# Two column blocks of a down projection as one unit of seven block products: a float32 decoder block on one core

## The chip, the cores and the metric

The kernel runs on one core of one Trainium2 chip. The metric is the device time of one execution in microseconds (us). The kernel before was run three times: 2167.27 us median, 2163.76 to 2168.08. A core has TensorE (PE, matrix products), VectorE (DVE, element by element), ScalarE (ACT, functions and copies with a scale), GpSimd (POOL) and SyncE (SP, here the queue that issues nearly all DMAs).

## The reference, cut to what matters

One decoder layer over 256 tokens of width 2048, in float32: a half-step FFN, a mixer (retention and sliding-window attention side by side), cross-attention into 256 memory tokens, a second half-step FFN, a final norm.

```
def swiglu(x, w_gate, w_up, w_down):
    return (jax.nn.silu(x @ w_gate) * (x @ w_up)) @ w_down
...
h = h + 0.5 * swiglu(rms_norm(h, ffn1_norm[l]), ffn1_w_gate[l], ffn1_w_up[l], ffn1_w_down[l])
n = rms_norm(h, mix_norm[l])
rq, rk, rv, rg, sq, sk, sv = jnp.split(n @ w_in[l], IN_SPLITS, axis=-1)
...
h = h + jnp.concatenate([ret, swa.astype(h.dtype)], axis=-1) @ w_out[l]
h = h + memory_cross_attention(rms_norm(h, xa_norm[l]), rms_norm(mem, mem_norm[l]), xa_wq[l], xa_wkv[l], xa_wo[l])
h = h + 0.5 * swiglu(rms_norm(h, ffn2_norm[l]), ffn2_w_gate[l], ffn2_w_up[l], ffn2_w_down[l])
return rms_norm(h, final_norm)
```

The inner width of an FFN is 5632, that is 11 blocks of 512; the model width is 4 blocks of 512.

## The kernel before, in words

**A product.** Each float32 operand is split into a high part (a rounded copy, made by ScalarE) and a low part (the rest, a subtraction on VectorE): `halves`, lines 74 to 77. `three` (lines 583 to 587) adds high x high, high x low and low x high into PSUM. The stationary operand is a 128x128 piece of the activations, the moving one a 128x512 piece of weights. The page's lines L585, L586 and L587 are these three matmuls, L72 the high part and L77 the low part of anything.

**Units and steps.** A `Unit` (lines 155 to 174) makes one block of 512 output columns for all 256 tokens. It goes over blocks of 512 of the inner dimension, two steps to a block; a step has two pieces of 128 rows, two halves of the tokens and three matmuls: 12 matmuls of 512 columns. All units stand in one list (`units`), and `run_stream` (lines 341 to 457) turns that list into one list of steps and runs it in order. `together` (lines 286 to 302) lets two neighbours run joined: both without their last block, then both last blocks. Ahead of each step the weights of the step three further on are split (`LOOKAHEAD`), and loads are issued up to four steps beyond that (`AHEAD`). Loads come by SP's queue, in the order of the program, into tiles `wf` (three buffers, each two steps); the splits lie in `wh` and `wl` (four buffers each).

**Twins and the seven products.** A `Twin` (lines 176 to 259) makes two blocks of columns, here gate and up of one FFN block, over the same activations. Three of the four inner blocks go by plain steps: 3 x 2 x 2 = 12. The fourth, number `SEVEN` = 3, is taken as 2x2 blocks (token half by rows) times 2x2 (rows by gate and up), which needs eight products by the rule and seven by a scheme of sums and differences: `prepare` (line 207) makes the differences of weights (L212) and their split, `multiply` (line 217) runs one of seven products of 6 matmuls; four of them use sums of activations (`sums_of`, lines 261 to 284; L277), and the results are put together by additions on VectorE (L238). The seven are put between the plain steps, from the third to the ninth. The two weight tiles of the fourth block ("wide") are `blk` tiles, 13 of which are shared by nearly everything else.

**The turn.** What a unit gives has tokens on partitions; the next product needs them on the free axis. `cross` (lines 556 to 575): VectorE transposes 32x32 pieces (L563) into a tile `t4k` (two buffers), one step later SP writes it to DRAM (`box`), two steps later GpSimd issues four reads back (L572), and `TURN` = 6 steps later a function receives the block: it makes halves of it, or adds it to the residual `hT` (L596). These delays count steps (`clock`; a product of the seven counts half): `later` puts a task in a list, and `run_due` runs it when its step comes. `run_until` runs tasks before their time when a step needs what they make.

**The FFN.** `ffn` (lines 612 to 663) goes over groups of blocks: all gate and up products of a group, then `down` for the group, which adds into the residual. The first block of an FFN (b = 0) is two units, the others are Twins. FFN1 has two groups, of 6 and 5 blocks; FFN2 has three, of 4, 4 and 3. `down` is four units, one for each block of columns, over the blocks of the group. FFN1's (`to_h`, lines 590 to 610) are scaled by 0.5 on ScalarE and crossed; FFN2's (lines 1105 to 1117) need no turn, since by then the residual has been turned back into two `blk` tiles (`turn_h`, line 1092), and they are added there by VectorE (L1116). A group's last block is due in the first down unit.

**Start.** PE runs a few products with the identity (L94, `WARM`) while the first loads are under way. The first 16 steps take a gate step and an up step in turn; the first weights come in pieces of 256 or 512 columns (lines 346 to 357).

## Time and profile before

| | |
|---|---|
| median of 3 runs | 2167.27 us (2163.76 to 2168.08) |
| the profiled execution | 2163.22 us |
| its span, first to last instruction | 2161.2 us |
| mean granted TensorE clock | 0.997 |
| busy share PE / DVE / ACT / POOL | 99% / 72% / 51% / 7% |
| matmuls | 9652 |
| read from HBM | 443.08 MB |

The profile shows one execution. Busy time of PE comes from modelled ends of pipelined matmuls, so a PE that is busy 99% needn't be at its best rate: the count of matmuls in a stretch says more. A line in the views is a line of the kernel; since helpers record most instructions, L72 and L77 stand for copies and splits of many tiles, and the tile's name (out<-in) tells which. The chain of waits gives start, length and who, each piece released by the one before it.

### The profile page before, as it was taken

Reading aid. Unit: us, or ns where it says so; the run is one execution under the profiler, and the core shown is the slowest. Engines: PE = TensorE matmul, PEld = TensorE weight load, DVE = VectorE, ACT = ScalarE, POOL = GpSimd, SP = SyncE. Lnnn points to the kernel's source line nnn. Section 1 sums busy time; section 2 is a strip of 40 time slices with the busy share of each in tenths; the row PEclk is TensorE's granted clock in tenths of the full one; section 3 lists DMA queues with packets and bytes.
Section 4 is the critical chain, followed back from the end, with each engine's and each line's share of the span. In section 5 each row is a group of like instructions: output and inputs, shape, how many; then the busy total and the mean of one; then the engine's idle time right before and its main releaser. Section 6 shows DMA issues by size and latency. Waiting matters only on the chain.

```text
span 2161.2 us, 25375 instructions
## 1 busy us (share of the span) xinstructions
PE 2142.7 (99%) x9652; PEld 1773.1 (82%) x9652; DVE 1548.7 (72%) x1827; ACT 1106.0 (51%) x1350; POOL 149.1 (7%) x257
## 2 busy tenths in 40 slices
PE   9999999999999999999999999999999999999998
PEld 7788888888888888888888888888888888888876
DVE  6888855688866678787675565567885688757865
ACT  6555544455545555646454544455554455535544
POOL 0000000000000010101111100010110000000000
PEclk9999999999999999999999999999999999999999
DMA  8666677666667566656867764585866566665663
GB/s 293 209 229 216 212 234 228 230 224 234 214 226 252 205 212 217 196 193 238 263 231 243 227 217 170 203 252 213 276 224 223 213 235 215 211 211 201 227 197 141
DMA packets 137531, 478.29 MB, mean 221 GB/s; under 512 B 11713, under 2 KB 12481, under 8 KB 137281
## 3 DMA queue, kind: packets, MB, share of 16 engines
q1 hardware_dynamic: 125600, 445.03, 58.9%
q0 software_dynamic: 11520, 31.47, 6.5%
q8 instruction: 75, 1.23, 0.2%
q14 instruction: 48, 0.39, 0.1%
q10 hardware_dynamic: 288, 0.18, 0.0%
HBM read 443.08 MB, written 33.55 MB: 221 GB/s over the span
## 4 chain that ended last, share of the span: by engine, by line
PE 92%; DMA 3%; DVE 2%; issue 1%; ACT 1%; POOL 0%; SPq 0%; ACTq 0%; POOLq 0%; DVEq 0%
PE acc L585 28%; PE acc L586 28%; PE acc L587 28%; DMA t4k<-box 2%; PE tmp L585 2%; PE tmp L586 2%; PE tmp L587 2%; DVE wl L77 1%; DMA wf<-in_w_in_rqk 0%; DMA box<-t4k 0%; POOL t4k L572 0%; DMA wf<-in_ffn_w_up 0%; PE tmp L810 0%; ACT blk L72 0%; PE tmp L791 0%
## 5 line engine op out<-in xcount | busy, mean ns | idle before, releaser
L77 DVE TENSOR_TENSOR wl<-wf,wh 128x1024 fp32r<-128x1024 f32 (+1 forms) x696 | 844.5, 1217 | 484.8 <-ACT wh L72 479.4
L72 ACT ACTIVATE wh<-wf 128x1024 fp32r<-128x1024 f32 (+1 forms) x696 | 732.0, 1055 | 809.7 <-PE acc L587 761.5
L585 PE MATMUL acc<-wh,blk 128*128 128x512 f32 (+1 forms) x2904 | 1131.3, 390 | 5.4 <-ACT blk L72 4.0
L586 PE MATMUL acc<-wl,blk 128*128 128x512 f32 (+1 forms) x2904 | 1128.8, 389 | 2.5 <-DVE wl L77 2.5
L587 PE MATMUL acc<-wh,blk 128*128 128x512 f32 (+1 forms) x2904 | 1128.2, 389 | 0.0
L585 PEld LDWEIGHTS acc<-wh,blk 128*128 128x128 f32 x2904 | 546.2, 188 | 121.8 <-ACT blk L72 5.4
L586 PEld LDWEIGHTS acc<-wl,blk 128*128 128x128 f32 x2904 | 546.3, 188 | 114.4 <-DVE wl L77 3.8
L587 PEld LDWEIGHTS acc<-wh,blk 128*128 128x128 f32 x2904 | 546.1, 188 | 112.7 <-DVE blk L77 0.6
L572 POOL DMA_DIRECT2D t4k<-box x240 | 138.6, 584 | 1790.6 <-DMA box<-t4k 549.7
L72 ACT ACTIVATE wh<-blk 128x1024 fp32r<-128x1024 f32 x140 | 148.3, 1060 | 78.4 <-PE acc L587 60.6
L77 DVE TENSOR_TENSOR wl<-blk,wh 128x1024 fp32r<-128x1024 f32 x140 | 170.6, 1218 | 8.7 <-ACT wh L72 3.2
L72 ACT ACTIVATE blk<-t4k 128x512 fp32r<-128x512 f32 (+3 forms) x84 | 46.6, 602 | 64.0 <-DMA t4k<-box 63.8
L212 DVE TENSOR_TENSOR blk<-blk,blk 128x1024 f32<-128x1024 f32 x60 | 73.4, 1224 | 1.4
L563 DVE STREAM_TRANSPOSE t4k<-t2k 128x512 f32<-128x512 f32 x88 | 57.7, 691 | 13.9 <-ACT t2k L72 13.8
L77 DVE TENSOR_TENSOR blk<-t4k,blk 128x512 fp32r<-128x512 f32 (+2 forms) x76 | 47.0, 659 | 24.9 <-ACT blk L72 24.2
L585 PE MATMUL tmp<-wh,blk 128*128 128x512 f32 x160 | 62.4, 390 | 0.0
L587 PE MATMUL tmp<-wh,blk 128*128 128x512 f32 x160 | 62.2, 389 | 0.0
L586 PE MATMUL tmp<-wl,blk 128*128 128x512 f32 x160 | 62.2, 389 | 0.0
L238 DVE TENSOR_TENSOR t2k<-t2k,acc 128x512 f32<-128x512 f32 x80 | 51.3, 683 | 6.8 <-PE acc L587 6.7
L238 DVE TENSOR_TENSOR t2k<-t2k,tmp 128x512 f32<-128x512 f32 x80 | 52.9, 682 | 0.7
L585 PEld LDWEIGHTS tmp<-wh,blk 128*128 128x128 f32 x160 | 30.2, 189 | 6.3
L586 PEld LDWEIGHTS tmp<-wl,blk 128*128 128x128 f32 x160 | 30.2, 189 | 6.3
(134 smaller groups left out, 728.1 us busy)
## 6 DMA issues: line engine op xcount, KB each, us to landing
wf<-in_ffn_w_down SPq DMA_DIRECT2D x88, 1024.0 KB, 4.9
wf<-in_ffn_w_gate SPq DMA_DIRECT2D x67, 1024.0 KB, 7.0
wf<-in_ffn_w_up SPq DMA_DIRECT2D x67, 1024.0 KB, 5.5
box<-t4k SPq DMA_DIRECT2D x60, 512.0 KB, 3.2
t4k<-box POOLq DMA_DIRECT2D x240, 128.0 KB, 6.4
blk<-in_ffn_w_gate SPq DMA_DIRECT2D x20, 1024.0 KB, 7.6
blk<-in_ffn_w_up SPq DMA_DIRECT2D x20, 1024.0 KB, 7.7
wf<-in_w_in_rqk SPq DMA_DIRECT2D x16, 1024.0 KB, 7.4
```

What stands on the lines that cost most here:

```text
L72: return nc.scalar.activation(dst, src, AF.Copy, **kw)
L77: nc.vector.tensor_tensor(lo, src, hi, ALU.subtract)
L212: nc.vector.tensor_tensor(src, a, b, ALU.subtract)
L238: nc.vector.tensor_tensor(out, a, b, ALU.add)
L563: nc.vector.transpose(z[:, t, :].rearrange("p (g q j) -> p q g j", g=4, q=4), squares_of(v))
L572: nc.gpsimd.dma_start(z[32 * g : 32 * g + 32].rearrange("p t (i n) -> p (t i) n", i=4), far[g])
L585: nc.tensor.matmul(o, ah, bh, start=start, stop=False)
L586: nc.tensor.matmul(o, ah, bl, start=False, stop=False)
L587: nc.tensor.matmul(o, al, bh, start=False, stop=stop)
```

## The change

- The Twin takes any pair of weight blocks, any list of plain blocks and any block for the seven products. The down products of the first two groups of each FFN become two Twins of two column blocks each, with the group's first block by seven products; the third group keeps four units, the first two of them joined.
- FFN1 goes over three groups (4, 4, 3), as FFN2 does.
- The sums of activations for those two blocks are made in the step that receives the block (`made`), and split there.
- Landing buffers `wf` become one pool of five (`big`) for pairs, wide tiles, the retention table, the keys of the window attention and two key blocks of the cross-attention; `blk` goes from 13 to 11. FFN2's residual lies in `hT` instead of two `blk` tiles.
- A turned block is received later in many places: 9 steps for FFN blocks below 10 and FFN1's adds of column blocks 0 to 2, 7 for block 10, 7 to 11 elsewhere. Window scores follow one step sooner after it.
- Start: the first steps take two gate steps and then two up steps; the first 1 MB lands as two transfers of 512 KB, and steps 0 and 1 multiply its halves of 256 columns, in 48 matmuls of 256 instead of 24 of 512. Seven warming products instead of nine; a Silu on a small tile at the very start.

```
-WARM = 9
+WARM = 7
...
+    def big(dt=F32):
+        return wpool.tile([P, 2, 1024], dt, tag="wf", name=nm("wf"), bufs=5)
...
+    early = sm(1, "ms")
+    nc.scalar.activation(early, mhalf[:, :1], AF.Silu)
...
-        def __init__(self, weights, index, norm, sums, done):
-            self.w = [w[2 * index : 2 * index + 2] for w in weights]
+        def __init__(self, weights, lhs, plain, seven, sums, done, pair=True):
+            self.w, self.lhs, self.plain, self.seven = weights, lhs, list(plain), seven
...
-            plain = [(b, f, i) for b in range(4) if b != SEVEN for f in range(2) for i in range(2)]
+            plain = [(b, f, i) for b in self.plain for f in range(2) for i in range(2)]
...
+        def load_wide(self, f):
+            x, c = big(), self.seven
+            if self.pair:
+                nc.sync.dma_start(x, self.w[f][:, c].rearrange("f p n -> p f n"))
+                x = x.rearrange("p f (k n) -> p k f n", n=S)
+            else:
+                nc.sync.dma_start(x, self.w[f][2 * c : 2 * c + 2].rearrange("c p n -> p c n"))
+                x = x.rearrange("p c (k f n) -> p (c k) f n", k=2, f=2)
+            self.wide.append(x)
...
         def first_sums(self):
-            p = self.products
-            self.u2 = self.add(t2k(), self.u1, p[5])
-            self.u3 = self.add(t2k(), self.u2, p[4])
+            self.u2 = self.add(t2k(), self.u1, self.products[5])
+            self.u3 = self.add(t2k(), self.u2, self.products[4])
+            self.u5 = self.add(t2k(), self.u3, self.products[3])
 
         def second_sums(self):
-            p5 = self.products[3]
-            self.u5 = self.add(t2k(), self.u3, p5)
-            self.u4 = self.add(self.u2, self.u2, p5)
+            self.u4 = self.add(self.u2, self.u2, self.products[3])
...
+    def split_sums(s):
+        z = blk().rearrange("p k c s -> p (k c s)").rearrange("p (c i j s) -> p c i j s", c=2, i=4, j=2)
+        halves(z[:, 0], z[:, 1], s)
+        return z
...
     def run_stream():
         steps = all_steps()
         steps[:FIRST] = [x for y in zip(steps[: FIRST // 2], steps[FIRST // 2 : FIRST]) for x in y]
+        steps[1], steps[2] = steps[2], steps[1]
...
+                wf = big()
+                load_x(0, 0, 2)
+                for f in range(2):
+                    nc.sync.dma_start(wf[:, f, :], steps[0][0].w[f, steps[0][3]])
+                load_x(0, 2, 4)
+                loaded[0] = loaded[1] = wf
+                loaded[2], loaded[3] = load_pair(steps[2][0].w, steps[2][3])
...
+        first_order = ((0, 0, 2), (1, 0, 2), (0, 2, 4), (1, 2, 4))
...
-    def to_h(w, lhs, factor, blocks, norm=None, then=None):
+    def to_h(w, lhs, factor, blocks, norm=None, then=None, spare=0, seven=None, sums=None):
...
+            cross(s, add, TURN + spare * (b < 3))
+        for b in range(4):
+            if seven is not None:
+                if b % 2 == 0:
+                    Twin(
+                        [w[2 * i : 2 * i + 2] for i in (b, b + 1)], lhs, [x for x in blocks if x != seven], seven, sums,
+                        lambda f, s, b=b: done(s, b + f, True),
+                    )
...
             def made(out):
                 acts[b] = halves_of(out, blk())
-            cross(s, made)
+                if b in starts:
+                    y = blk(F32).rearrange("p k c s -> p (k c s)")[:, :1024].rearrange("p (i j s) -> p i j s", i=4, j=2)
+                    sums_into(y, lambda t, k: out[t][:, k::2])
+                    asums[b] = split_sums(y)
+            cross(s, made, TURN + (3 if b < 10 else 1))
...
-    ffn(n1, a["ffn1_w_gate"], a["ffn1_w_up"], ffn1_down, (range(0, 6), range(6, 11)))
+    def ffn1_down(g, acts, fbs, sums):
+        if g < 2:
+            to_h(a["ffn1_w_down"], acts, 0.5, fbs, spare=3, seven=fbs[0], sums=sums)
+        else:
+            to_h(a["ffn1_w_down"], acts, 0.5, fbs, nmix, near_mix, spare=3)
+            units[-4].then = units[-3]
+    ffn(n1, a["ffn1_w_gate"], a["ffn1_w_up"], ffn1_down, (range(0, 4), range(4, 8), range(8, 11)))
...
-                    st["swa_at"] = max(st.get("swa_at", 0) + SWA_EVERY, clock[0] + 3)
+                    st["swa_at"] = max(st.get("swa_at", 0) + SWA_EVERY, clock[0] + 2)
...
-            cross(rs, turned)
+            cross(rs, turned, TURN + 1)
...
+    def ffn2_down(g, acts, fbs, sums):
+        w, done = a["ffn2_w_down"], (first_down, first_down, last_down)[g]
+        for nb in range(0, 4, 2) if g < 2 else ():
+            Twin(w[nb : nb + 2], acts, fbs[1:], fbs[0], sums, lambda f, s, nb=nb: done(nb + f, s), pair=False)
+        for nb in range(4) if g == 2 else ():
+            if nb == 3:
+                Unit(w, 3, 512, acts, very_last, fbs, per_half=True)
             else:
+                Unit(w, nb, 512, acts, lambda acc, nb=nb: done(nb, [acc[:, t, :] for t in range(2)]), fbs)
+            if nb == 1:
+                together()
```

More of the change, by code (lines that the diff above doesn't have):

```diff
@@ L36 @@
 SWA_EVERY = 5
-SEVEN = 3
 @with_exitstack
@@ L58, in blk @@
     def blk(dt=F32R):
-        return work.tile([P, 4, 2, S], dt, tag="blk", name=nm("blk"), bufs=13)
+        return work.tile([P, 4, 2, S], dt, tag="blk", name=nm("blk"), bufs=11)
+    def big(dt=F32):
+        return wpool.tile([P, 2, 1024], dt, tag="wf", name=nm("wf"), bufs=5)
     def t2k(dt=F32):
@@ L379, in fetch, with split_first, some, multiply_first @@
                     loaded.update(enumerate(load(u.w, piece, 1 + two), at))
+        first_order = ((0, 0, 2), (1, 0, 2), (0, 2, 4), (1, 2, 4))
+        def split_first(wf):
+            parts = [[wpool.tile([P, 1024], F32R, tag=x, name=nm(x)) for x in ("wh", "wl")] for _ in range(2)]
+            def some(f, lo, hi):
+                cs = slice(lo * S, hi * S)
+                halves(parts[f][0][:, cs], parts[f][1][:, cs], wf[:, f, cs])
+            n1.some(0, [hT[0][:, :2, :]], 0)
+            some(0, 0, 1)
+            some(0, 1, 2)
+            some(1, 0, 2)
+            n1.some(0, [hT[0][:, 2:, :]], 2)
+            some(0, 2, 4)
+            some(1, 2, 4)
+            return [[x.rearrange("p (k n) -> p k n", n=S) for x in y] for y in parts]
+        def multiply_first(u, x, parts, orders):
+            for f, lo, hi in orders:
+                for k in range(lo, hi):
+                    for t in range(2):
+                        ts = slice(t * P, (t + 1) * P)
+                        wh, wl = (y[:, k, :] for y in parts[f])
+                        three(
+                            u.acc[t][:, t, f * S : (f + 1) * S], x[:, k, 0, ts], x[:, k, 1, ts], wh, wl,
+                            f == 0 and k == 0, False,
+                        )
         def prepare(upto):
@@ L435, in run_stream @@
             wh, wl = ready.pop(at)
-            if at == 0:
-                for i, k in enumerate(ks):
-                    for t in range(2):
-                        by_tokens(u, u.acc[t], x, wh[:, i : i + 1, :], wl[:, i : i + 1, :], [k], t, first and i == 0, False)
+            if at < 2:
+                multiply_first(u, x, (wh, wl), first_order[2 * at : 2 * at + 2])
             else:
@@ L587, in three, with done @@
         nc.tensor.matmul(o, al, bh, start=False, stop=stop)
-    def to_h(w, lhs, factor, blocks, norm=None, then=None):
-        def done(acc, b):
+    def to_h(w, lhs, factor, blocks, norm=None, then=None, spare=0, seven=None, sums=None):
+        def done(s, b, fresh=False):
+            if factor != 1.0:
+                s = [(x, x if fresh else t2k()) for x in s]
+                s = [copy(y, x, scale=factor) and y for x, y in s]
             def add(out):
@@ L601, in add @@
                     then(b)
[L602 to L610 removed]
+            cross(s, add, TURN + spare * (b < 3))
[5 more added lines that the diff above has]
+                        lambda f, s, b=b: done(s, b + f, True),
+                    )
+            else:
+                Unit(w, b, 512, lhs, lambda acc, b=b: done([acc[:, t, :] for t in range(2)], b), blocks, pair=True)
     def ffn(norm, w_gate, w_up, down, groups):
@@ L656, in ffn @@
                 if b > 0:
-                    Twin((w_gate, w_up), b, norm, sums, both_done(b))
+                    Twin([w[2 * b : 2 * b + 2] for w in (w_gate, w_up)], norm.blocks, range(3), 3, sums, both_done(b))
                     continue
@@ L877, in finish @@
                     for i in range(4):
-                        later(4 + i // 2, lambda i=i: ret_scores(g, i, qk))
-            cross([acc[:, t, :] for t in range(2)], finish)
+                        later(3 + i // 2, lambda i=i: ret_scores(g, i, qk))
+            cross([acc[:, t, :] for t in range(2)], finish, TURN + 1)
         return done
@@ L945, in turned @@
                 mixT[g] = x
-            cross(ret, turned)
+            cross(ret, turned, TURN + 3 * (g == 0))
             if g == 1:
@@ L1001, in made @@
             def made(out):
-                dst[i] = halves_of(out, blk())
+                if dst is keys and i < 2:
+                    x = big(F32R).rearrange("p f n -> p (f n)").rearrange("p (k c s) -> p k c s", k=4, c=2)
+                else:
+                    x = blk()
+                dst[i] = halves_of(out, x)
                 if then is not None:
                     later(1, then)
-            cross(s, made)
+            cross(s, made, TURN + 2)
         return done
@@ L1092, in turn_h @@
     def turn_h(b):
-        if b == 0:
-            h.extend(blk(F32).rearrange("p k c s -> p (k c s)") for _ in range(2))
         def made(out):
             for t in range(2):
-                copy(squares_of(h[t][:, b * 512 : (b + 1) * 512]), out[t])
-        cross([hT[b][:, :, t * P : (t + 1) * P].rearrange("p q (a j) -> p q a j", a=4) for t in range(2)], made)
+                copy(squares_of(h(t, b * 512, 512)), out[t])
+        cross([hT[b][:, :, t * P : (t + 1) * P].rearrange("p q (a j) -> p q a j", a=4) for t in range(2)], made, TURN + 5)
     def squares(part, src):
```

164 lines of the change are left out of this document (68 added, 96 removed).

## The prediction

> **What bounds the kernel now.** I read the page first, then the busy time by stretches, then the chain of waits where a stretch held too few matmuls.
>
> ```profile
> span 2161.2 us, 25375 instructions
> PE 2142.7 (99%) x9652; PEld 1773.1 (82%) x9652; DVE 1548.7 (72%) x1827; ACT 1106.0 (51%) x1350; POOL 149.1 (7%) x257
> PE 92%; DMA 3%; DVE 2%; issue 1%; ACT 1%; POOL 0%; SPq 0%; ACTq 0%; POOLq 0%; DVEq 0%
> ```
>
> TensorE (PE) carries 92% of the chain that ended last, so the length of its instruction list sets the time, and the rest is the few places where it stops. The stretches below (us, busy us and count of each engine, granted clock, DMA share) tell both.
>
> ```profile
> core 0: us, PE busy (x) PEld busy (x) DVE busy (x) ACT busy (x) POOL busy (x), PEclk, DMA share, GB/s
> 100.00:200.00 100.00, 100.00 (x443) 82.80 (x443) 87.54 (x90) 52.92 (x56) 6.90 (x12) 1.00 0.66 221
> 60.00:100.00 40.00, 37.88 (x159) 30.67 (x158) 31.99 (x34) 21.19 (x23) 2.47 (x4) 0.96 0.68 236
> 1600.00:1640.00 40.00, 39.42 (x174) 32.23 (x173) 28.00 (x32) 19.00 (x22) 4.60 (x8) 1.00 0.78 253
> 1860.00:1900.00 40.00, 39.61 (x175) 32.37 (x174) 26.53 (x30) 18.02 (x19) 2.30 (x4) 1.00 0.66 221
> 2080.00:2120.00 40.00, 37.00 (x157) 30.05 (x156) 23.54 (x26) 15.82 (x20) 2.30 (x4) 0.96 0.64 208
> 1480.00:1525.00 45.00, 45.00 (x200) 37.28 (x199) 39.11 (x43) 28.86 (x34) 4.64 (x8) 1.00 0.65 231
> 1525.00:1567.00 42.00, 42.00 (x187) 34.59 (x186) 36.73 (x39) 23.47 (x27) 4.60 (x8) 1.00 0.77 246
> 0.00:14.00 14.00, 11.44 (x46) 9.41 (x47) 6.18 (x13) 8.21 (x15) 0.70 (x6) 1.00 0.88 285
> ```
>
> In an undisturbed stretch 443 matmuls of 512 columns take 100 us: 0.2257 us each. That is the price of a matmul here (its busy span in the table is longer because matmuls overlap). A plain step is 12 of them, 2.71 us. By that rate 40 us hold 177.2, so the four stretches of 40 us lost 18, 3, 2 and 20 matmuls' time: 4.1, 0.7, 0.5 and 4.6 us (each to about one matmul, 0.2). The chain of waits names what each was. The first and the last:
>
> ```profile
> 63.05 9.57 DMA t4k<-box
> 72.72 0.64 ACT blk L72
> 77.00 0.50 PE acc L586
> ...
> 2082.13 1.29 DVE t2k L238 x2
> ...
> 2091.34 9.29 DMA t4k<-box
> ...
> 2100.73 0.64 ACT blk L72
> 2101.41 0.50 PE acc L585
> ```
>
> Both are a block that goes out to DRAM and back to be turned (`cross`). At 72.72 ScalarE stood at the copy that needs the returned block, with the splits of later weights queued behind it; the VectorE half of those splits starved, and PE with it. At 2101.41 PE itself needed the block.
>
> **Fewer products.** A down unit over four blocks has 8 plain steps, so two units have 16 x 12 = 192 matmuls. As a Twin they have 12 plain steps and 7 products of 6: 144 + 42 = 186. FFN1 and FFN2 each have two groups with two such Twins: 8 x 6 = 48 matmuls, 48 x 0.2257 = **-10.8 us**. Going from two to three groups in FFN1 adds no matmul; it adds four evacuations of a column block on other engines. PE is the bound in all these stretches, so this comes off the end if VectorE keeps up:
>
> ```profile
> L77 DVE TENSOR_TENSOR wl<-wf,wh 128x1024 fp32r<-128x1024 f32 (+1 forms) x696 | 844.5, 1217 | 484.8 <-ACT wh L72 479.4
> L212 DVE TENSOR_TENSOR blk<-blk,blk 128x1024 f32<-128x1024 f32 x60 | 73.4, 1224 | 1.4
> L238 DVE TENSOR_TENSOR t2k<-t2k,acc 128x512 f32<-128x512 f32 x80 | 51.3, 683 | 6.8 <-PE acc L587 6.7
> L563 DVE STREAM_TRANSPOSE t4k<-t2k 128x512 f32<-128x512 f32 x88 | 57.7, 691 | 13.9 <-ACT t2k L72 13.8
> L596 DVE TENSOR_TENSOR h<-h,t4k 128x512 f32<-128x512 f32 x32 | 20.6, 685 | 7.1 <-DMA t4k<-box 7.1
> L277 DVE TENSOR_TENSOR blk<-blk 128x256 f32<-128x256 f32 x8 | 3.0, 415 | 0.0
> L72 ACT ACTIVATE blk<-blk 128x1024 fp32r<-128x1024 f32 x2 | 2.1, 1052 | 1.5 <-DVE blk L277 1.5
> ```
>
> A down Twin's VectorE work: 19 splits x 1.22 + 4 differences of weights x 1.22 + 8 sums x 0.68 = 33.5 us; FFN1 adds 4 transposes and 4 additions to h, 5.5, so 39.0; FFN2 adds 4 additions from the last row's like, 2.7, so 36.2. PE needs 186 x 0.2257 = 42.0. A gate-and-up Twin is the nearest row that exists: 1525 to 1567 is one, VectorE busy 36.7 of 42, PE without a gap. So the down Twins cost **0** beside PE; the other end is 1 us for each of the four in FFN1. ScalarE is at 23.5 of 42 there and isn't late.
>
> **The sums of activations.** The first block of a group gets four sums of 128x256 (4 x 0.415) and a split (1.05 on ScalarE, then 1.22 on VectorE) in the step that receives it: 3.9 us in which VectorE is kept from weight splits. In the groups that begin with a Twin (block 4) three steps of lead (8.1 us) cover it. In the first Twin of each FFN the sums of the norm's block are made too, and VectorE is nearly full: 39.1 of 45 us from 1480 to 1525, 32.0 of 40 with the wait from 60 to 100. I take 1.0 us for each of these two, ends 0 and 3.9.
>
> **Waits that get more room.** ScalarE's row at the first place (in brackets how long it had stood, and for whom):
>
> ```profile
> 72.72 1.15 ACT L72 ACTIVATE blk<-t4k 128x512 fp32r<-128x512 f32 x2 [5.35 <-DMA t4k<-box]
> ```
>
> In FFN1's first Twin the block is now received 9 steps after its unit, not 6: 3 x 2.71 = 8.1 us later in ScalarE's queue, more than the 5.35 that it stood. The 4.1 us go: **-4.1 + 1.0 = -3.1** with the burst above. In FFN2's third group the first down unit ran 4 plain steps (10.9 us) before it needed block 10; the two units joined run 8 (21.7 us). From the last sums at 2082.13 to the landing at 2100.63 (2091.34 + 9.29) are 18.5 us, so it fits by 3.2. In the other two groups the late block now comes after 8 plain steps and 6 products (29.8 us). **-4.6 -0.7 -0.5 = -5.8.** Next late there is nothing that the trace shows. FFN2's first Twin **+1.0**.
>
> **Start of the mixer.** Two small stops:
>
> ```profile
> 777.79 0.62 PE L765 MATMUL tmp<-blk,blk 128*128 128x256 f32 x3 [0.35 <-DVE blk L77]
> 807.94 0.50 PE L586 MATMUL acc<-wl,blk 128*128 128x512 f32 x1 [0.61 <-DVE wl L77]
> ```
>
> The turned queries are received one step later and their scores follow one step sooner, so the sum is unchanged; only the queue behind is freer. **-0.5**, ends -1.0 and 0. Against it stands FFN1's end: its adds now wait 9 steps, and three crossings, of units that end 2 and 6 steps apart, share two turning buffers (`t4k`), so the third goes out about half a step late and its block is needed some 8 steps after its unit: 21.7 us against the same 18.5 plus 1.4. Margin 1.8, and landings scatter: **+0.5**, ends 0 and +3.
>
> **Start.** Before, two waits for small loads:
>
> ```profile
> 4.29 0.63 ACT L72 ACTIVATE wh<-wf 128x512 fp32r<-128x512 f32 x1 [1.27 <-DMA wf<-in_ffn_w_gate]
> 9.15 1.15 ACT L72 ACTIVATE wh<-wf 128x512 fp32r<-128x512 f32 x2 [2.64 <-DMA wf<-in_ffn_w_up]
> L94 PE MATMUL tmp<-ident 128*128 128x128 f32 x18 | 4.2, 430 | 1.4 <-POOL ident masks.py:199 1.4
> 78.46 0.63 PE L585 MATMUL acc<-wh,blk 128*128 128x512 f32 x1
> 78.89 0.63 PE L586 MATMUL acc<-wl,blk 128*128 128x512 f32 x1
> ```
>
> By 14 us 28 products had run (46 less 18 warming ones). Now the first product needs 0.75 MB instead of 0.38 (a 256 KB piece of x and 512 KB of weights): at the 285 GB/s of this stretch some 1.3 us later. In return the second unit's weights are needed only after two steps, so the wait of 2.64 goes. Estimate **-0.4**; low end -1.3. The high end is the clock: after the pause at 75 us products came 0.43 us apart, not 0.23, and the stretch's granted clock is 0.96 of 40 us, that is 3.2 us at half. A slow window costs 8 x 0.2 = 1.6 us. Warming shrinks from 4.2 to 14/18 of it, 3.3 us, so such a window may cover the first products: high end +1.7. The Trainium skill's page "TensorE: Matmul & The Clock Gate", Part 1, says that the clock is let up only after about 3.4 us of sustained work and falls again after an idle window of that length. The second half differs from this trace, where less than 3.4 us of standing still brought the half rate. By the first half the shorter warming falls just short, which would make the start +1.7 and the total 2.1 us worse.
>
> **Sum.** -10.8 - 3.1 - 5.8 + 1.0 - 0.5 + 0.5 - 0.4 = **-19.1 us**. The profiled execution took 2163.22 us (2161.2 of span and 2.0 around it), so one like it would take 2144.1. The median of the three runs, 2167.27, lies 4.05 above it, and the predicted time is for a median: 2167.27 - 19.1 = **2148** us.
>
> **Rivals.** (1) *VectorE becomes the bound.* For it: 88 of 100 us in Twins, 39.0 of 42.0 by my count in FFN1's. Against: no gap of PE in any such stretch. Both first Twins at 3.9 (+5.8) and four down Twins at 1 (+4): -9.3, 2158. It decides from 42 us of VectorE in a Twin. (2) *The waits come back elsewhere*, since a block still takes 18.5 us to return and the two `t4k` buffers are now held longer. Then the 4.1, 5.8 and 0.5 are not won: -8.7, 2158.6. (3) *Slower: one pool of five landing buffers.* The two wide tiles of a Twin and the pairs of plain steps had buffers of their own; now a pair can find the pool full until the seventh product's split frees a wide tile, and the queue that issues loads (SP) stands there with all later loads and box writes behind it.
>
> ```profile
> wf<-in_ffn_w_up SPq DMA_DIRECT2D x67, 1024.0 KB, 5.5
> blk<-in_ffn_w_up SPq DMA_DIRECT2D x20, 1024.0 KB, 7.7
> ```
>
> A load takes 5.5 to 7.7 us to land and is issued 7 steps ahead, so it must lose about four plain steps before PE stops. If each of the 28 Twins (20 gate-and-up, 8 down) stops for one step, that is 28 x 2.71 = +76 - 19 = 2224; it decides from 19.1 / 28 = 0.7 us a Twin. Against it: by the order in the code, when a Twin's fourth pair is fetched two wide tiles and one pair are held, so two are free. That the products are not saved cannot be: the count is fixed by the code.
>
> **How the numbers follow.** My sum has 0.76, VectorE 0.12, returned waits 0.07, the pool 0.05. The likeliest gives 2148. Low end: every gain at its best (-10.8 - 4.1 - 5.8 - 1.0 - 1.3 = -23.0) on the profiled execution, 2140; high end: rivals 1 and 2, 2158.6, and the start at its worst, 2160. This leaves out the pool and a little on either side. Measured differences under 0.2% (4.3 us) can't be told from none. Faster takes the sum and most of rivals 1 and 2, 0.91; slower the pool, 0.05; the rest is the same, 0.04.
>
> **What would show it.** Matmuls of 512 columns fall by 48 net of the first two steps (24 of 512 become 48 of 256); the first FFN Twin has no lone wait of ScalarE for `t4k`; granted clock 1.00 in all stretches but the first and last; PE of a down Twin 42.0 us with VectorE at 36 to 39. I am wrong if PE idles in the down Twins on `wl`, or waits on `wf` from the pool.

## The result and the profile after

The changed kernel took 2147.37 us (median of 4 runs, 2143.3 to 2150.31), the kernel before 2165.52 us (4 runs, 2163.19 to 2168.08): ratio 0.9915, 95% interval 0.9893 to 0.9936. Median against median that is -18.2 us; the profiled execution of after took 2148.38 us, against 2163.22 before, -14.8. One execution of the changed kernel (in e0 below) took 5569.52 us where all its others took 2143 to 2154, and is left out of every figure here. The forecast (2148, a sum of -19.1) was right in sign and size, and its sum some 1 to 5 us too large: the later runs of both kernels (before 2162.46 and after 2148.60, in e0) give -13.9. The small difference hides two larger ones, as the traces show: the predicted gains came nearly whole, and new waits took some of them back.

First the page of after: span, busy time, and the shares of the chain that ended last.

```profile
span 2146.2 us, 25612 instructions
PE 2129.7 (99%) x9624; PEld 1764.9 (82%) x9624; DVE 1664.5 (78%) x1984; ACT 1144.4 (53%) x1395; POOL 159.1 (7%) x273
PE 57%; DVE 2%; DMA 2%; issue 1%; ACT 0%; POOL 0%; POOLq 0%; ACTq 0%; DVEq 0%
```

The chain couldn't be followed to its start this time (the shares add up to 62%), so the 57% is not to be held against the 92% of before. VectorE rose by 116 us of busy time and TensorE's span fell: no contradiction, since VectorE had that time free. The same stretches as before, with a down Twin (178 to 220) and, at the end, three new ones (columns as in the prediction):

```profile
0.00:14.00 14.00, 11.06 (x67) 9.99 (x68) 7.13 (x16) 9.28 (x19) 0.70 (x6) 1.00 0.87 329
60.00:100.00 40.00, 40.00 (x178) 33.14 (x177) 37.65 (x43) 23.36 (x26) 1.76 (x4) 1.00 0.69 230
178.00:220.00 42.00, 42.00 (x187) 34.76 (x186) 36.91 (x40) 22.94 (x24) 2.30 (x4) 1.00 0.59 201
1480.00:1525.00 45.00, 45.00 (x201) 37.24 (x200) 43.15 (x51) 28.10 (x33) 4.63 (x8) 1.00 0.71 228
1600.00:1640.00 40.00, 40.00 (x178) 33.14 (x177) 34.91 (x37) 24.07 (x28) 4.61 (x8) 1.00 0.73 236
1860.00:1900.00 40.00, 40.00 (x178) 33.14 (x177) 34.90 (x37) 20.64 (x21) 2.32 (x4) 1.00 0.67 222
2080.00:2120.00 40.00, 40.00 (x178) 33.10 (x178) 23.68 (x26) 19.41 (x25) 2.17 (x4) 1.00 0.68 241
720.00:760.00 40.00, 38.21 (x185) 32.22 (x184) 29.36 (x48) 19.21 (x27) 3.17 (x4) 0.96 0.45 150
1030.00:1070.00 40.00, 38.45 (x165) 31.49 (x164) 25.35 (x30) 16.96 (x20) 3.38 (x6) 0.96 0.71 219
1450.00:1480.00 30.00, 29.04 (x130) 23.80 (x129) 15.30 (x20) 15.27 (x19) 1.62 (x1) 1.00 0.76 264
```

The four stretches of 40 us that held 159, 174, 175 and 157 matmuls now hold 178 each, a full list: the stops that were to go are gone. 178 to 220 is a down Twin of FFN1: 42.0 us without a gap of TensorE, VectorE at 36.9; over all eight down Twins VectorE is at 34.6 to 37.0 of 42 us. From 1480 to 1525 VectorE reaches 43.15 of 45 us (the sums of the norm's block are in it) and TensorE still has no gap. The last three lines are the other side: stretches around 733, 1044 and 1464 us where TensorE stops. What it waited for, by the view of waits, TensorE only (us in total, times, the longest). Before:

```profile
PE acc L585 <- ACT blk L72: 4.0, 3, 3.0
PE acc L586 <- DVE wl L77: 2.5, 3, 1.6
PE acc L585 <- ACT wh L72: 1.5, 2, 1.0
```

After:

```profile
PE tmp L568 <- DVE t2k L565: 4.3, 3, 1.8
...
PE acc L632 <- ACT wh L74: 1.2, 2, 1.0
PE acc L633 <- DVE wl L79: 1.0, 2, 0.7
```

The waits for a returned block (`blk`) are gone, and a kind has come that the kernel before lacked: L568 is the tiny product with a column of ones that adds up a norm's squares, L565 the last addition on VectorE that it needs. The three norms are those after FFN1, after the mixer (the memory's norm) and after the cross-attention.

To account for all of it I take each section from one norm's product to the next and subtract what its matmuls take at their undisturbed spacing (0.2267 us from start to start with 512 columns, in both kernels). FFN2, for example, from 1467.80 to 2152.00 before and from 1465.21 to 2137.28 after, is 684.2 and 672.1 us; its matmuls are 677.3 and 671.8 us; so 6.9 and 0.2 us were lost.

| section, us lost by TensorE | before | after |
|---|---|---|
| start, from the first product at 1.37 to the first norm's at 46 | 4.70 | 4.50 |
| FFN1 | 4.87 | 2.37 |
| mixer, to the memory norm | 7.57 | 10.00 |
| to the next norm | 0.12 | 1.74 |
| cross-attention | 0.29 | 1.92 |
| FFN2 | 6.92 | 0.23 |
| after the last product | 9.16 | 8.95 |

The matmuls themselves fell by 11.0 us, the losses by 3.9: -14.9. Around the norms 7.6 us appeared: 1.95 at 733, then 2.4, 1.6 and 1.6 in the three sections that follow (the half clock behind 733 among them). Everything else fell by 22.6.

### The profile page after: what moved, and what is told of

It reads as the page before. It is cut to its first block, busy times and chain, and to the rows that moved or that the text cites. A ratio compares the mean times of both kernels' runs of the same rounds, so it can differ in the third digit from the quotient of the medians.

```text
span 2146.2 us, 25612 instructions
## 1 busy us (share of the span) xinstructions
PE 2129.7 (99%) x9624; PEld 1764.9 (82%) x9624; DVE 1664.5 (78%) x1984; ACT 1144.4 (53%) x1395; POOL 159.1 (7%) x273
## 4 chain that ended last, share of the span: by engine, by line
PE 57%; DVE 2%; DMA 2%; issue 1%; ACT 0%; POOL 0%; POOLq 0%; ACTq 0%; DVEq 0%
PE acc L633 17%; PE acc L632 17%; PE acc L634 17%; DMA t4k<-box 2%; PE tmp L634 2%; PE tmp L632 2%; PE tmp L633 2%; DVE wl L79 1%; DVE h L647 0%; PE tmp L866 0%; POOL t4k L619 0%; DVE t4k L610 0%; PE tmp L847 0%; DVE blk L520 0%; DMA box<-t4k 0%
## 5 line engine op out<-in xcount | busy, mean ns | idle before, releaser
L74 ACT ACTIVATE wh<-wf 128x1024 fp32r<-128x1024 f32 (+1 forms) x861 | 905.9, 1056 | 884.5 <-PE acc L634 819.5
L79 DVE TENSOR_TENSOR wl<-wf,wh 128x1024 fp32r<-128x1024 f32 (+1 forms) x861 | 1037.9, 1215 | 373.4 <-ACT wh L74 357.6
L632 PE MATMUL acc<-wh,blk 128*128 128x512 f32 (+1 forms) x2832 | 1100.6, 389 | 1.2 <-ACT wh L74 1.2
L633 PE MATMUL acc<-wl,blk 128*128 128x512 f32 (+1 forms) x2832 | 1099.1, 388 | 1.1 <-DVE wl L79 1.0
L634 PE MATMUL acc<-wh,blk 128*128 128x512 f32 (+1 forms) x2832 | 1098.1, 388 | 0.0
L632 PEld LDWEIGHTS acc<-wh,blk 128*128 128x128 f32 x2832 | 533.0, 188 | 112.2 <-ACT wh L74 2.4
L634 PEld LDWEIGHTS acc<-wh,blk 128*128 128x128 f32 x2832 | 532.9, 188 | 108.7
L222 DVE TENSOR_TENSOR wf<-wf,wf 128x1024 f32<-128x1024 f32 x84 | 102.6, 1222 | 1.9
L632 PE MATMUL tmp<-wh,blk 128*128 128x512 f32 x224 | 87.1, 389 | 0.0
L634 PE MATMUL tmp<-wh,blk 128*128 128x512 f32 x224 | 87.1, 389 | 0.0
L634 PEld LDWEIGHTS tmp<-wh,blk 128*128 128x128 f32 x224 | 42.0, 188 | 8.7
L632 PEld LDWEIGHTS tmp<-wh,blk 128*128 128x128 f32 x224 | 42.0, 188 | 8.7
L74 ACT ACTIVATE blk<-t4k 128x512 fp32r<-128x512 f32 (+2 forms) x72 | 39.2, 596 | 7.5 <-DMA t4k<-box 7.5
L647 DVE TENSOR_TENSOR h<-h,t4k 128x512 f32<-128x512 f32 x40 | 25.8, 687 | 16.6 <-DMA t4k<-box 16.6
```

Source lines behind the costliest of these rows:

```text
L74: return nc.scalar.activation(dst, src, AF.Copy, **kw)
L79: nc.vector.tensor_tensor(lo, src, hi, ALU.subtract)
L222: nc.vector.tensor_tensor(src, p, q, ALU.subtract)
L632: nc.tensor.matmul(o, ah, bh, start=start, stop=False)
L633: nc.tensor.matmul(o, ah, bl, start=False, stop=False)
L634: nc.tensor.matmul(o, al, bh, start=False, stop=stop)
```

## Why TensorE waits at the norms: reading the trace

Three groups of rows around 1044 us. TensorE in after:

```profile
1045.93 0.62 PE L568 MATMUL tmp<-ones,t2k 128*128 128x1 f32 x4 [1.55 <-DVE t2k L565]
...
1047.42 0.63 PE L632 MATMUL acc<-wh,blk 128*128 128x512 f32 x1
1047.84 0.63 PE L633 MATMUL acc<-wl,blk 128*128 128x512 f32 x1
```

After the pause products come 0.42 us apart, not 0.227: the granted clock is halved, and eight products at that pace cost 1.6 us more. VectorE in after, then in before:

```profile
1037.11 1.29 DVE L647 TENSOR_TENSOR h<-h,t4k 128x512 f32<-128x512 f32 x2 [3.64 <-DMA t4k<-box]
...
1042.00 1.30 DVE L610 STREAM_TRANSPOSE t4k<-acc 128x512 f32<-128x512 f32 x2
...
1045.46 0.42 DVE L565 TENSOR_TENSOR t2k<-t2k 128x256 f32<-128x256 f32 x1
```

```profile
1042.42 1.29 DVE L596 TENSOR_TENSOR h<-h,t4k 128x512 f32<-128x512 f32 x2 [1.41 <-DMA t4k<-box]
```

VectorE stood 3.64 us (1.41 before) at the addition to the residual, for a turned block that was still on its way; behind it in its queue are the weight splits and the next transposes, and at the end of the queue the norm's sum at 1045.46, for which TensorE waited. And why the block was late: SP's queue in after, in before, and in the first experiment below, where the wide tiles have a pool of their own. Each shows the write of the block to DRAM and the loads issued behind it (start, time over which they were issued).

```profile
1019.32 0.37 SPq L614 DMA_DIRECT2D box<-t4k  x1
1019.77 5.37 SPq L333 DMA_DIRECT2D wf<-in_w_out  x4
```

```profile
1026.86 0.37 SPq L567 DMA_DIRECT2D box<-t4k  x1
1027.96 17.28 SPq L312 DMA_DIRECT2D wf<-in_w_out  x4
```

```profile
1018.10 0.37 SPq L617 DMA_DIRECT2D box<-t4k  x1
1019.21 16.67 SPq L336 DMA_DIRECT2D wf<-in_w_out  x4
```

With five buffers in one pool, where no Twin needs wide tiles, four loads of 1 MB go out within 5.4 us right behind the write, where three buffers spread them over 17. The median landing of these loads is 8.0 us in after against 5.5 in before:

```profile
wf<-in_w_out SPq DMA_DIRECT2D x16, 1024.0 KB, 8.0
```

```profile
wf<-in_w_out SPq DMA_DIRECT2D x16, 1024.0 KB, 5.5
```

In that stretch of after the four reads of the block land 6.1 to 9.0 us after their issue, beside loads that take 8.5 to 16.8; in before it is 5.8 to 7.1, beside loads of 5.9 to 7.8.

**Theory A**, then: the common pool lets loads go out in bursts, the crossing that shares the DMA engines with them returns late, VectorE stands, and the norm's sum is late. **Rival B**, in the expectations below: more crossings share two turning buffers, whatever the loads do. **Rival C**, there: the waits only move, or cost the same wherever the norm's sum stands. Two more: **rival D**, the down Twins and the joined units themselves, by VectorE's load or the order of the work, and **rival E**, the delays, since blocks are received later. At 733 us the suspects are B and E from the start: there the third crossing's write went out late, for want of a turning buffer.

## Experiments

Each of the three sets ran on one chip with its own runs of the kernel before: 2162.46 us for e0 to e3, 2163.17 for e4 to e7, 2161.62 for e8 to e11. Times are medians; in brackets the ratio to before with its 95% interval.

**e0: after, unchanged.**

> The changed kernel as it is, as the mark for the three beside it: 2143 to 2150 us like its four runs so far. In its profile the products with the column of ones (the end of a norm's statistic) should again be preceded by waits of 1 to 2 us near 733, 1044 and 1464 us, two of them followed by a stretch at half the clock.

2148.60 us (0.9932, 0.9913 to 0.9952). The view of waits has L568 with 5.8 us over three times: these pauses are no accident of one execution.

**e1: two pools.** Three buffers for pairs, two for wide tiles and what else took one.

```
     def big(dt=F32):
-        return wpool.tile([P, 2, 1024], dt, tag="wf", name=nm("wf"), bufs=5)
+        return wpool.tile([P, 2, 1024], dt, tag="wf", name=nm("wf"), bufs=3)
+    def wide(dt=F32):
+        return wpool.tile([P, 2, 1024], dt, tag="wd", name=nm("wd"), bufs=2)
...
-            x, c = big(), self.seven
+            x, c = wide(), self.seven
```

> The five landing buffers as two pools again, three for loads and two for the wide tiles, the table and the keys; all else as changed. Theory A (five common buffers let SP issue loads in bursts, so blocks that go out to DRAM and back land later, VectorE stands at their addition and the norm's small product comes late): the three waits before the norm's products shrink to under 0.5 us each with their half-clock windows, loads of w_out land in about 5.5 us instead of 8.0, the total falls by 5 to 8 us against the changed kernel. Rival B (the waits come from more crossings sharing two turning buffers, whatever the loads do): waits and total stay within 2 us.

2143.72 us (0.9911, 0.9891 to 0.9931), 4.9 below e0. The waits at 1044 and 1464 are gone; one of 0.9 stays at 733. The stretch around 1044 and the line of L571 (the same product) in the view of waits:

```profile
1030.00:1070.00 40.00, 40.00 (x180) 33.00 (x179) 26.41 (x30) 17.94 (x20) 5.32 (x9) 1.00 0.77 244
```

```profile
PE tmp L571 <- DVE t2k L568: 0.9, 1, 0.9
```

180 matmuls and full clock, against 165 and 0.96, with the `w_out` loads spread again and landing in 5.5 us. That splitting the pool takes these two waits away is shown, and rival B, which expected no change, falls for them; the path by the late crossing is read from the rows above, and the table behind e11 shows how far it holds.

**e2: the two norms two steps later, one pool.** If the norm's sum is only late, more room hides it.

```
-    nmem = Norm(G_MEM, "nmem", 7)
+    nmem = Norm(G_MEM, "nmem", 9)
...
-    n2 = Norm(G_FFN2, "n2", 4)
+    n2 = Norm(G_FFN2, "n2", 6)
```

> The end of the statistic of the memory norm and of FFN2's norm comes two steps later in the program. Both theories: the waits at 1044 and 1464 us go (1.7 + 1.6 of half clock + 1.1), the one at 733 stays, total 3 to 5 us lower than the changed kernel. Rival C (those waits only move to whatever PE does next): no change within 1 us.

2142.70 us (0.9906, 0.9887 to 0.9924), 5.9 below e0. The view of waits keeps only the one at 733:

```profile
PE tmp L568 <- DVE t2k L565: 2.4, 1, 2.4
```

So by the medians of e1 and e2 the two waits cost 5 to 6 us, with what half clock follows them (3.6 in e0's trace, 4.5 in after's), and either remedy takes them; rival C falls with that. But at 1044 it was not only more room that helped: the burst is there as in after, and yet VectorE stood 0.88 us for the block instead of 3.64.

```profile
1020.30 5.37 SPq L333 DMA_DIRECT2D wf<-in_w_out  x4
1034.87 1.29 DVE L647 TENSOR_TENSOR h<-h,t4k 128x512 f32<-128x512 f32 x2 [0.88 <-DMA t4k<-box]
```

**e3: down by units, one pool.** The Twins of the down products undone, all else kept.

```
-        starts = [x[0] for x in groups[:2]]
+        starts = []
...
-            to_h(a["ffn1_w_down"], acts, 0.5, fbs, spare=3, seven=fbs[0], sums=sums)
+            to_h(a["ffn1_w_down"], acts, 0.5, fbs, spare=3)
+            units[-4].then = units[-3]
...
-        for nb in range(0, 4, 2) if g < 2 else ():
-            Twin(w[nb : nb + 2], acts, fbs[1:], fbs[0], sums, lambda f, s, nb=nb: done(nb + f, s), pair=False)
-        for nb in range(4) if g == 2 else ():
+        for nb in range(4):
```

> Down products by eight instead of seven in every group: units of one column block, in every group the first two of them joined, no sums of activations; all else as changed. By the count of matmuls it is 48 x 0.2257 = 10.8 us slower than the changed kernel, 2156 to 2161 us. If VectorE, fuller with Twins, costs PE anything in the down stretches, the difference is smaller than 10.

2153.17 us (0.9954, 0.9937 to 0.9972): only 4.6 above e0, where 10.8 was expected. Read by sections, the matmuls are back (nominal time +10.9 against after), but the losses fell from 20.8 to 14.9 us (without the last row of the table), because the norms' waits shrank to a single 0.5:

```profile
PE tmp L568 <- DVE t2k L565: 0.5, 1, 0.5
```

So the run does not price the Twins by itself. That the waits shrink with the pool untouched speaks for rival D as a second condition: the pool's bursts hurt where the rest of the order leaves a crossing no slack. Which part of the order gave it slack here I haven't settled.

**e4 and e5: the same comparison with two pools.** e4 is e1 with e2's delays, and with one unit of the window's queries moved ahead of the keys' to give the first norm room; e5 is e1 with e3's units.

```
e4:
-    nmix = Norm(G_MIX, "nmix", 3, spread=True)
+    nmix = Norm(G_MIX, "nmix", 4, spread=True)
...
+    Unit(a["w_in_sq"], 0, 512, nmix.blocks, sq_done(0), range(4))
     Unit(a["w_in_skv"], 0, 256, nmix.blocks, skv_done, range(4))
-    for g in range(2):
-        Unit(a["w_in_sq"], g, 512, nmix.blocks, sq_done(g), range(4))
-        if g == 0:
-            together()
+    together()
+    Unit(a["w_in_sq"], 1, 512, nmix.blocks, sq_done(1), range(4))
```

> Two pools, the two norms' ends two steps later, and at the mixer's start the first query unit ahead of the key-value unit, so that the mixer norm's end can come one step later too. Theory A with the late-addition mechanism: none of the three waits before the norms' products is left (the 1.1 us that stayed at 733 with two pools goes), 2140 to 2143 us, 1 to 2 below two pools alone. Rival C (a wait of VectorE for the returned block costs PE the same wherever the norm's end stands): equal to two pools alone, 2143 to 2145.

> Two pools and the down products by units of eight products, the first two joined in every group. With the waits of the norms out of the way in both, the price of the 48 matmuls alone is left: 10.8 us more than two pools with Twins, 2153 to 2156 us. If the down Twins cost PE something that the common pool's waits hid, the difference is nearer to the 4.4 us that one pool showed: 2147 to 2150.

e4 2142.23 us (0.9899, 0.9883 to 0.9916), e5 2153.67 (0.9956, 0.994 to 0.9972): 11.4 apart on the same chip, and e5 is 9.95 above e1. The 48 matmuls at 10.8 us lie between: this prices the Twins (e5 differs from e1 in them alone; it still waits 1.4 us for a norm's sum near 740, e1 0.9). e4 itself gained little over e1: no norm's sum is waited for, but TensorE stopped at the unit behind the joined pair instead, until ScalarE had copied their results out (`t2k`):

```profile
744.58 0.50 PE L635 MATMUL acc<-wh,blk 128*128 128x512 f32 x1 [1.72 <-ACT t2k L77]
```

**e6: back to six steps before a block is received in the FFNs** (and no spare steps for FFN1's additions).

```
-            cross(s, made, TURN + (3 if b < 10 else 1))
+            cross(s, made)
...
-            to_h(a["ffn1_w_down"], acts, 0.5, fbs, spare=3, seven=fbs[0], sums=sums)
+            to_h(a["ffn1_w_down"], acts, 0.5, fbs, seven=fbs[0], sums=sums)
...
-            to_h(a["ffn1_w_down"], acts, 0.5, fbs, nmix, near_mix, spare=3)
+            to_h(a["ffn1_w_down"], acts, 0.5, fbs, nmix, near_mix)
```

> The changed kernel with FFN blocks and FFN1's column blocks received 6 steps after their unit again. If the room of 9 steps is what removed the stop in FFN1's first Twin, a stop of 2 to 4 us with a stretch at half the clock comes back between 70 and 85 us, and total is 2 to 6 us above the changed kernel. Rival: the stop went by the earlier Silu table and the other start, and stays away.

2144.76 us (0.9914, 0.9898 to 0.9931): 2.6 us faster than the first runs of after and 3.8 than e0, where I had expected slower. Two surprises in one run. At FFN1's end the write of the third crossing went out at 694.75 us instead of 698.10, as the turning buffers are freed three steps sooner, and the wait at 733 is gone (there rival E is borne out); 1.3 us of the other two stays. And in the first Twin the 4.1 us of before did not come back, though ScalarE stands for the block again. ScalarE, and the stretch:

```profile
69.96 1.15 ACT L74 ACTIVATE blk<-t4k 128x512 fp32r<-128x512 f32 x2 [2.64 <-DMA t4k<-box]
```

```profile
60.00:100.00 40.00, 39.64 (x176) 32.50 (x175) 36.81 (x42) 23.09 (x25) 2.35 (x4) 1.00 0.65 226
```

It stands 2.64 us instead of 5.35, and TensorE loses 0.5 us at full clock. So the nine steps account for at most 0.5 of the 4.1 us: without them the rest stays away too.

**e7: loads issued two steps ahead of the splits, not four, one pool.** Meant as another way to break the bursts.

```
-AHEAD = 4
+AHEAD = 2
```

> One pool of five as changed, but loads issued two steps less ahead. Theory A in its sharper form (it is the number of loads in flight that delays the returned blocks, not which buffer they take): the waits before the norms' products shrink as with two pools, w_out lands in under 7 us, total 2142 to 2146. If the pool matters in another way: no change, 2147 to 2150. If loads come too late now: PE waits on wf and it is slower than 2150.

2164.53 us (1.0004, 0.999 to 1.0017). All of the gain is gone, but for another reason: TensorE now starves for split weights.

```profile
PE acc L633 <- DVE wl L79: 6.9, 13, 0.9
PE acc L632 <- ACT wh L74: 5.0, 4, 3.3
PE tmp L568 <- DVE t2k L565: 3.8, 3, 3.1
```

Of the norms' waits the two near 741 and 1056 shrink to 0.4 us each, and the one near 1478 grows to 3.1 although VectorE doesn't stand for the block there; the edit was too blunt to tell about theory A.

**e8: two pools, later norms, and no spare steps in FFN1's last group.**

```
e1 and e2, and
-            to_h(a["ffn1_w_down"], acts, 0.5, fbs, nmix, near_mix, spare=3)
+            to_h(a["ffn1_w_down"], acts, 0.5, fbs, nmix, near_mix)
```

> Two pools, the memory norm's and FFN2's norm's ends two steps later, and FFN1's last group received after 6 steps instead of 9, so that its third crossing doesn't wait for a turning buffer. If the 1.1 us at 733 that two pools left come from that buffer, it goes, and the total is 2140 to 2143 us, below the changed kernel by 5 to 7 and by about 20 below the kernel before. If it comes from the loads alone, the wait stays near 1 us and the total is that of two pools, 2143 to 2145.

2141.57 us (0.9901, 0.9881 to 0.992), 20 below the kernel before; by the ratio it is level with e4, and these two are the fastest. No norm is waited for; what TensorE waits for in the whole kernel, and the first of the three stretches (at 1030 to 1070 it is 180 matmuls again):

```profile
PE tmp L100 <- POOL ident masks.py:199: 1.4, 1, 1.4
PE acc L636 <- DVE wl L82: 1.3, 1, 1.3
PE acc L635 <- ACT wh L77: 1.1, 1, 1.1
PE tmp L824 <- DVE blk L82: 0.5, 1, 0.5
```

```profile
720.00:760.00 40.00, 40.00 (x192) 33.16 (x191) 28.22 (x46) 20.62 (x28) 3.05 (x5) 1.00 0.55 192
```

**e9: e6 without the early Silu.** Besides the nine steps, the change calls a Silu once at the very start, so that ScalarE has loaded its table before it is needed in the first FFN unit. This run asks whether that is where the 4.1 us went.

```
-    early = sm(1, "ms")
-    nc.scalar.activation(early, mhalf[:, :1], AF.Silu)
```

> 6 steps everywhere in the FFNs as in the run with turns of 6, and the early Silu taken out, so the table is loaded in ScalarE's way at the first gate's end again (1.28 us). If the table is what made FFN1's first stop 0.5 us instead of 4.1, the stop returns with 1.5 to 4 us near 78, possibly with a half-clock window. If the stop went with the start, the groups or the luck of the landing, it stays under 1 us.

2148.60 us (0.9936, 0.9921 to 0.9951), 3.8 above e6, or 4.8 by the ratios to before (0.0022 x 2162). ScalarE now stands 3.74 us for the first block, and TensorE's two stops in the stretch cost 1.5 us where e6 has one of 0.5:

```profile
50.70 1.28 ACT L672 ACT_TABLE_LOAD   x1 [2.46 <-PE acc L632]
...
72.09 1.16 ACT L74 ACTIVATE blk<-t4k 128x512 fp32r<-128x512 f32 x2 [3.74 <-DMA t4k<-box]
```

```profile
60.00:100.00 40.00, 38.84 (x170) 31.49 (x169) 36.67 (x42) 22.46 (x25) 2.47 (x4) 1.00 0.70 240
```

The table load of 1.28 us lies ahead of the unit's end and delays the block; it explains about 1 us of the 4.1. The other part of the stop, and the half clock behind it, stay away in this run too, with six steps and without the early table, and the traces show where it went: from the issue of its write to the landing of its last read the block was 15.6 us on its way before, 14.0 in e9 and 13.9 in e6, its last read landing after 9.6, 8.2 and 8.1 us. That fits ScalarE's standing: 5.35 us before, 3.74 in e9 with the shorter way, 2.64 in e6 without the table's load too. The load of the gate's weights issued beside it landed after 9.4 us before and 6.6 in both; which of the changes at the start made the way shorter is not settled. (The rest of the difference to e6 is 0.8 us at the start and longer waits at the norms.)

**e10: no joined units** in FFN2's third group and in FFN1's.

```
             to_h(a["ffn1_w_down"], acts, 0.5, fbs, nmix, near_mix, spare=3)
-            units[-4].then = units[-3]
...
-            if nb == 1:
-                together()
```

> The changed kernel with the first two down units of the last group of each FFN run one after the other. In FFN2 block 10 is then due after 4 plain steps instead of 8: a stop of 3 us and a half-clock window of 1.6 us come back near 2085, as before; in FFN1's last group likewise 3 to 5 us near 665. Total 4 to 9 us above the changed kernel. If 7 steps of delay for block 10 alone were enough, nothing returns.

2152.03 us (0.9949, 0.9934 to 0.9964), 3.4 above e0's time and 3.7 by the ratios. TensorE stops 3.6 us near 659 and 3.0 us at 2089; the second in the timeline:

```profile
2092.28 0.50 PE L632 MATMUL acc<-wh,blk 128*128 128x512 f32 x1 [2.83 <-ACT blk L74]
```

It is the same wait for the group's last block that the kernel before had at 2101. The join removes it, as forecast. By sections FFN1 lost 4.1 us more than in e0 and FFN2 3.2, while the mixer lost 2.9 less, since the norms' waits shrank to 1.2 in all; so the total understates what the joins are worth.

**e11: three turning buffers, one pool** (paid for by two fewer `t2k`).

```
-        return work.tile([P, 512], dt, tag="t2k", name=nm("t2k"), bufs=7)
+        return work.tile([P, 512], dt, tag="t2k", name=nm("t2k"), bufs=5)
...
-        z = work.tile([P, 2, 512], F32, tag="t4k", name=nm("t4k"), bufs=2)
+        z = work.tile([P, 2, 512], F32, tag="t4k", name=nm("t4k"), bufs=3)
```

> Three turning buffers instead of two, paid for with two of the seven small tiles; all else as changed. If the third crossing of FFN1's last group is late because it waits for a buffer, it goes out some 3 us sooner and the wait at 733 shrinks to under 1 us, while the waits at 1044 and 1464 stay. Fewer small tiles may cost something elsewhere: total 2143 to 2152.

2144.28 us (0.9914, 0.9897 to 0.9931). The third crossing's write is at 694.38 us and the wait at 733 is gone with all spare steps kept: without the want of a turning buffer it doesn't come (two pools alone, with the write as late as 698.12, left 0.9). The wait at 1044 is gone as well, which theory A doesn't say; only the one near 1458 is left:

```profile
PE tmp L568 <- DVE t2k L565: 1.7, 1, 1.7
```

Nor does the third buffer explain it: the block that VectorE stands for was transposed 6.43 us behind the one before it in after and in e11 alike, so nothing held it up there. The traces of all the runs, at the addition near 1037 and at the last one ahead of 1464 (us; the way is from the issue of the block's write to its addition):

| runs | pools | way | VectorE stood | TensorE then waited | VectorE stood near 1456 |
|---|---|---|---|---|---|
| after, e0, e9 | one | 17.8 to 18.0 | 3.6 to 3.8 | 1.6 to 1.7 | 3.2 to 3.8 |
| e6 | one | 17.2 | 3.1 | 1.0 | 2.6 |
| e3, e10 | one | 16.8, 16.7 | 2.6 | 0.5 | 0.7, 3.0 |
| e7 | one | 16.6 | 2.0 | 0.4 | 0 |
| e11 | one | 15.3 | 1.1 | 0 | 4.0 |
| e2 | one | 15.0 | 0.9 | 0 (norm later) | 3.4 |
| e1, e4, e5 | two | 15.0 to 15.4 | 0.8 to 1.3 | 0 | 0 |
| e8 | two | 16.9 | 2.7 | 0 (norm later) | 0 |
| before | its own | 15.6 | 1.4 | 0 | 2.1 |

Near 1456 the pool decides in all but two: with one pool VectorE stands 2.6 to 4.0 us (not in e3 and e7), with two it never does. At 1044 it doesn't decide alone. In every run with one pool the four loads go out within 5.5 us behind the write, and mostly the way is longer than with two; but in e2 and e11 the block is back as soon as in e1, and in e8 it is late without a burst. What else makes it late is not shown. What follows from a late block is: the longer VectorE stands, the longer TensorE waits, unless the norm's sum stands later, as in e8. The rows at 1464 show a delay that is handed on (VectorE in after):

```profile
1433.95 1.29 DVE L647 TENSOR_TENSOR h<-h,t4k 128x512 f32<-128x512 f32 x2 [2.93 <-DMA t4k<-box]
...
1440.42 1.31 DVE L610 STREAM_TRANSPOSE t4k<-acc 128x512 f32<-128x512 f32 x2
...
1456.00 1.29 DVE L647 TENSOR_TENSOR h<-h,t4k 128x512 f32<-128x512 f32 x2 [3.22 <-DMA t4k<-box]
...
1464.74 0.42 DVE L565 TENSOR_TENSOR t2k<-t2k 128x256 f32<-128x256 f32 x1
```

It stands 2.93 us, the next block's transposes behind it in the queue start the later, and then it stands 3.22 us for that block.

## Why the prediction was right, step by step

- **Fewer products, -10.8**: right. The count is as forecast, TensorE's nominal time fell by 11.0, and e4 against e5 and e1 against e5 price it at 11.4 and 9.95 on the chip. (The 0.2257 us of a matmul came from a count of 443 in 100 us; from start to start it is 0.2267, which changes the term by 0.05.) VectorE's 36.9 to 37.0 of 42 us in six of the eight down Twins lie in the 36 to 39 that were given, the 34.6 in the other two below, and rival 1 (VectorE as the bound) fell: no such stretch has a gap.
- **The sums of activations, +1.0 twice**: too high; 0 each. VectorE at 43.15 of 45 us still kept ahead.
- **FFN1's first Twin, -4.1**: right in size, by luck as far as the reason goes. The prediction put it down to a block received nine steps after its unit instead of six; e6 keeps six and loses 0.5 us. About 1 us is the early table load (e9), which the prediction listed nowhere as a cost or a gain; behind the rest is a way through DRAM that is 1.6 us shorter, for a reason that is open.
- **FFN2's waits, -5.8**: right. The section lost 6.7 us less (with its sums of activations at 0), and e10 brings the last of these waits back by undoing the join.
- **FFN1's end, +0.5 (0 to +3)**: the right place and mechanism, mis-sized. The third crossing left 3.35 us late (698.10 against 694.75 in e6), not 1.4, and the wait was 1.95 us in after and more in e0. e6, e8 and e11 each remove it by freeing a buffer.
- **Start of the mixer, -0.5**: its first stop (the scores' product, 0.35 us) is gone from the list of waits in after, but back with 0.5 in e0; the rest can't be told apart in a section that grew by 2.4 us for another reason.
- **Start, -0.4**: -0.2. The +1.7 that a slow window was to bring did not come in after, where full clock began at 5.33 us (6.32 before). The page "TensorE: Matmul & The Clock Gate", Part 1, of the Trainium skill would by its warm-up of 3.4 us have left the shorter warming just short; here 3.35 us of warming was enough, and in e2 and e3 full clock came 2.95 us after the first product, though in other runs 3.35 wasn't enough (last section).
- **The sentence that failed** is "Next late there is nothing that the trace shows". The norms' sums were next. Nothing waited there before, so no row named them, but VectorE's idle 1.41 us for a returned block at 1042 was a warning: the norm's sum stood behind it in the same queue. The prediction weighed the common pool only in rival 3, as too few buffers for a load (TensorE on `wf`, which never happened). What it did was the opposite: where no Twin runs, five buffers let more loads out at once than three, and the crossings shared the way with them (with the limits of the table behind e11). Rival 2 (waits come back elsewhere) is what partly occurred, at 7.6 us instead of 10.4.
- **The clock**: 1.00 was forecast for all stretches but the first and the last; it was 0.96 at 720 to 760 and at 1030 to 1070, behind two of the new pauses.

In sum: new waits of 7.6 us where 0.5 was allowed for (+7.1), the two sums of activations not paid (-2.0), and some 0.9 us more won in FFN2 turn the -19.1 into about the -14.9 of the two traces. That 2148 came within 0.6 us of the median is in part luck: it starts from 2167.27, the median of three runs, and all later runs of the kernel before have medians of 2161.62 to 2163.17.

## What to carry to other kernels

A shared pool of landing buffers is also a throttle on loads: making it larger where its other users are idle lets bulk loads out in a burst, and a small round trip through DRAM that a later step needs can pay for it. When a stop is removed, follow each engine's queue behind the wait that is left, even if nobody stood for it in the trace of before. And price a removed part on top of a version whose other waits are gone (e4 and e5), since undoing it alone (e3) moves those waits too.

## What the runs showed of the hardware

The granted clock after a pause doesn't follow from the pause's length alone. In the middle of a run half clock lasted 3.41 us each time, and once twice that (e7, 6.83). It followed pauses of 1.72 and 1.95 us (after, 1044 and 733), 1.9 (e11, 1459), two of 0.65 and 1.9 close together and one of 3.2 (before), 2.65 (e0), 3.6 (e10, 659), 3.3 and 3.5 (e7); none followed pauses of 1.73 (e9), 1.74 and 1.87 (e0), 1.88 (e4), 2.58 (e2, 733) and 3.0 (e10, 2089). The Trainium skill's page "TensorE: Matmul & The Clock Gate", Part 1, gives about 3.4 us of idleness for the fall; the window's length agrees with these traces, the length of the pause doesn't.

What fits is the pause's place. In each trace all moments at which the granted clock changes lie on one grid of 3.4133 us, to within 0.004 us: half clock begins at 735.78 and 1046.39 in after (310.61 apart, 91 steps), at 78.00 and 2102.10 in before (2024.10, 593 steps), at 793.51 and 1479.59 in e7 (686.08, 201 steps). I added up, for each window of this grid from 20 us on, how long TensorE stood in it, with a norm's four products of one column (0.45 us) counted as standing. Ahead of every half-clock window it was 2.1 us or more, in all other windows 2.0 or less. The 3.0 us of e10 lie across a border, 1.54 and 1.46, and so do the 2.58 of e2 and the 1.87 of e0; the 1.72 of after lie in one window, with 0.43 of the norm's products behind them. No run moved a pause on the grid on purpose.

At the start the place matters too: full clock began at 4.3 to 6.3 us in before, after, e0 to e3, e7, e9 and e10, but only at 9.7 to 10.4 in e4, e5, e6, e8 and e11, for which the start lost 5.1 to 5.7 us instead of 4.3 to 4.8 (5.9 in e9, where a half-clock window came back at 8.54; in e4, e9 and e11 the first product behind the warming came 0.7 to 0.9 us later than in after as well). Differences of a microsecond between kernels of this kind can come from that alone.
